# A matmul–bias–ReLU–matmul kernel: all block sums of y on VectorE, one product passed to the next through PSUM

## The chip, the cores and the metric

The kernel runs on one core of a Trainium2 chip. The core has five engines that run side by side, each through its own queue in order: TensorE (PE; its weight loads are shown apart as PEld), VectorE (DVE), ScalarE (ACT), GpSimd (POOL) and SyncE (SP), which issues most of the transfers. The metric is device time in microseconds for one execution. Before the change the median of three runs is 971.6 us (971.56 to 972.17).

## The reference

With x of 16 × 512 × 768, w1 of 768 × 3072, b1 of 3072 and w2 of 3072 × 768, all drawn at random in fp32:

```python
y = np.matmul(x, w1) + b1
y = np.maximum(y, 0)
return np.matmul(y, w2).astype(np.float32)
```

The 16 × 512 rows are one matrix of 8192 rows. The hidden width 3072 lies between the two products.

## The kernel before

**Tiling.** The rows are cut into 8 blocks of 1024 (`NSB`), the hidden width into 2 halves (`NCH`). So there are 16 iterations: 0 to 7 do the first half of the hidden width for the eight row blocks, 8 to 15 the second half, whose results are added in HBM to those of the first by accumulating DMAs that GpSimd issues. Operands are fp16, sums in PSUM fp32.

**First product, m1.** Each iteration forms y from x and w1 in six groups t = 0 to 5 (`first`, lines 524 to 583). A group is a 2 × 2 block product done in seven products instead of eight (Strassen–Winograd form): p1, p2, p6, p5, p7, p3, p4. Each is 3 matmuls of 128 × 512, so an iteration has 126 of them (line 537). The sums of x that they need (`sums_x`: slots XS1, XS2, XS4) and those of w1 (`sums_w1`: T1 to T4) are made ahead. Between the products ScalarE copies running sums with the bias to the SBUF tile `s` (`copy`, line 545: slots s1 = 0, s2 = 1 or 2, s5 = 4), and VectorE adds a bank to such a copy, clamps at 0 and writes y (`add`, line 549). p4 goes through ScalarE's Relu alone (line 579). Banks: kind "a" has three PSUM banks, "b" two, "c" three, and the group number picks the one. p6, p7 and p4 go on summing in p1's bank, p3 in p5's. Iteration 0 has a plain form of eight products instead (`first_plain`).

**Second product, m2.** Each iteration forms the output block from y and w2 in 20 products (`second`, list `SECOND`), each 8 matmuls of 128 × 384 (line 596). Products work on 20 blocks of y, of which 12 come out of m1 and the others are sums of blocks, and on 18 blocks of w2 and its sums. The y sums are eight instructions per quarter s of the columns (`sums_y`, line 458, two blocks each, 128 × 512 in all), four quarters. The quarters are complete after groups 1, 2, 4 and 5. Results go through ScalarE (line 612) and VectorE (line 618) into four output buffers `o` and to HBM. The same tile `s` holds m2's sums; its slot 4 is `s4`, last read by the 20th product's total, o6.

**Order.** All is written out by hand in one list (`run`, lines 699 to 726): each step has a key, and the steps are issued in the order of their keys. A group's seven steps have keys two apart and groups start seven apart, so the last three steps of a group lie between the first four of the next. m2's 20 steps follow two apart; its first step lies before the last two steps of group 5, and its last step after the first step of the next iteration's group 0. After every step up to two instructions are taken from the list `fill` (one during m2, unless more than eight wait), which holds the y sums of quarters 2 and 3, and then the step's `hooks` run, which `plan` fills: sums of x and w, squares for a range check (`stat_w1`, `stat_w2`, `square_x`), loads and stores.

**Where the y sums run.** `group_done` sends quarters 0 and 1 to GpSimd (`sums_y_aside`; in iteration 0 to VectorE) and quarters 2 and 3 through `fill` to VectorE. In iteration 7 the three sums of x for iteration 8 run on GpSimd (line 776). w1's sums run on GpSimd: in iteration 0 for the first half (24 instructions, lines 747 and 749), in iterations 1 to 6 for the second half, one group each, in borrowed x slots (`ahead_w1`). w2's 16 sums (`sum_w2`, line 329) run on VectorE and one of them on ScalarE.

Of the kernel before, what the change touches and what calls it, by code (L numbers as in the profile page):

```python
# [18 lines left out]
P = 128  # L19
# [130 lines left out]
class Fast:  # L150
# [32 lines left out]
    def __init__(self, ctx, tc, xf, w1, b1, w2, of):  # L183
        self.tc, self.nc = tc, tc.nc
        self.xf, self.w1, self.b1, self.w2, self.of = xf, w1, b1, w2, of
        self.M, self.K = xf.shape
        self.H, self.N = w2.shape
        self.NH = self.N // 2
        self.NSB = self.M // (2 * self.MH)
        self.NIT = self.NCH * self.NSB  # L190
        assert self.K == 6 * P and self.H == self.NCH * 2 * self.TP * P

        def pool(name, bufs, **kw):
            return ctx.enter_context(tc.tile_pool(name=name, bufs=bufs, **kw))
# [16 lines left out]
        self.w2dram = self.dram.tile([P, 6, 4, self.NH], FP16, name="w2d")  # L211
# [97 lines left out]

    def fetch_w2(self, slot, n=2):  # L310
        self.nc.sync.dma_start(out=self.v[:, slot:slot + n], in_=self.w2dram[:, slot:slot + n])

    def fetch_w2_aside(self, q):
        w = self.raw_pool.tile([P, 2, 4, self.NH], FP16, name="w2r", tag="raw")
        self.nc.sync.dma_start(out=w, in_=self.w2dram[:, 2 * q:2 * q + 2])
        self.w2_raw[2 * q], self.w2_raw[2 * q + 1] = w[:, 0], w[:, 1]

    def sum_w2(self, n):
# [3 lines left out]
        def block(slot):  # L322
            return self.w2_raw.get(slot, self.v[:, slot])

        if i is None:
            self.nc.scalar.activation(out=self.v[:, o], in_=block(j), func=ACTF.Copy,
                                      scale=float(sign))
        else:
            self.nc.vector.tensor_tensor(out=self.v[:, o], in0=block(i), in1=block(j),  # L329
                                         op=ALU.add if sign > 0 else ALU.subtract)  # L330
# [44 lines left out]

    def sums_x(self, it, which, engine=None):

        x = self.x.rearrange("p a k m -> p a (k m)")
        a11 = 4 * (it % 2)
        a12, a21, a22 = a11 + 1, a11 + 2, a11 + 3  # L380
        tt = (engine or self.nc.vector).tensor_tensor
        if which == 0:
            tt(out=x[:, self.XS1], in0=x[:, a21], in1=x[:, a22], op=ALU.add)
        elif which == 1:
            tt(out=x[:, a21:self.XS2 + 1:self.XS2 - a21],
               in0=x[:, a21:self.XS1 + 1:self.XS1 - a21],
               in1=x[:, a11:a11 + 1].to_broadcast((P, 2, 3 * self.MH)), op=ALU.subtract)
        else:
            tt(out=x[:, self.XS4], in0=x[:, a12], in1=x[:, self.XS2], op=ALU.subtract)

# [55 lines left out]

    def sums_y(self, n, s0, s1, engine=None):

        outs, ins0, ins1, sign = SUMS_Y[n]
        w = (s1 - s0) * self.QM  # L450

        def pair(i, j):
            cols = slice(s0 * self.QM, s1 * self.QM)
            if i == j:
                return self.y[:, i:i + 1, cols].to_broadcast((P, 2, w))
            return self.y[:, i:j + 1:j - i, cols]

        (engine or self.nc.vector).tensor_tensor(  # L458
            out=pair(*outs), in0=pair(*ins0), in1=pair(*ins1),
            op=ALU.add if sign > 0 else ALU.subtract)  # L460

    def group_done(self, it, t):

        def put(s0, s1, engine):
            self.fill += [lambda n=n: self.sums_y(n, s0, s1, engine) for n in range(8)]

        if t == 1:
            self.sums_y_aside(0, it)
        elif t == 2:
            self.sums_y_aside(1, it)  # L470
        elif t == 4:
            put(2, 3, self.nc.vector)
        elif t == 5:
            put(3, 4, self.nc.vector)

    def sums_y_aside(self, s, it):
        for n in range(8):
            self.sums_y(n, s, s + 1, self.nc.gpsimd if it else self.nc.vector)

    def first_plain(self, t):  # L480
# [34 lines left out]
        def last():  # L515
            step("a", m2, b2, 1, 1)
            self.group_done(0, t)

# [5 lines left out]
    def first(self, it, t):  # L524
# [22 lines left out]
        def add(half, m, ps, name):  # L547
# [3 lines left out]
                                  s1=0.0)  # L551

        def p1():
# [23 lines left out]
        def p4():  # L577
            mm(g["a"], xa22, self.T4, False)
            nc.scalar.activation(out=self.y_of(t, 1), in_=self.two(g["a"]), func=ACTF.Relu,  # L579
                                 bias=bias1)  # L580
            self.group_done(it, t)

        return [p1, p2, p6, p5, p7, p3, p4]


# [85 lines left out]
    def run(self):  # L671
# [42 lines left out]
        for _, n, i in sorted(keys):  # L714
# [13 lines left out]
    def plan(self):  # L728

        TP, NSB, NIT = self.TP, self.NSB, self.NIT  # L730
        self.hooks = {}
        pool = self.nc.gpsimd

# [14 lines left out]
        for t in range(TP):  # L748
            put("p1", 0, 5, 3, lambda t: self.sums_w1(self.w1s[t], (3,)), t)
        for n in range(len(SUMS_W)):  # L750
            put("p1", 0, 4 + n // 8, n % 8 // 2, self.sum_w2, n)

        for it in range(NIT):
            nxt = it + 1
            if nxt < NSB:
                for half in range(2):
                    if it:
                        put("m1", it, 1 + half, 0, self.transpose_x, nxt, half)
                    for s in range(4):
# [4 lines left out]
                put("m2", it, 0, 16, self.save_x, nxt, 0)  # L764
                put("m2", it, 0, 16, self.save_x, nxt, 1)
            elif nxt < NIT:
                put("m1", it, 0, 0, self.fetch_x, nxt, 0)
                if nxt > NSB:
                    put("m2", it, 0, 1, self.fetch_x, nxt, 1)
            if nxt < NSB:  # L770
                for n in range(3):
                    put("m2", it, 0, 8 + 2 * n, self.sums_x, nxt, n)

        last = NSB - 1
        for n in range(3):
            put("m2", last, 0, 1, self.sums_x, NSB, n, pool)
        for t in range(TP):
            for step, i in enumerate((0, 3, 8)):
                put("m2", 1 + t, 0, 1 + i, self.ahead_w1, 1 + t, t, step)
            put("m1", last, t, 6, self.fetch_w1, t)  # L780
        for n in range(12):
            put("m1", 1 + n // 3, 3 + n % 3, 0, self.load_w2,
                self.w2dram[:, n // 4 * 2:n // 4 * 2 + 2], 1, n // 4, n % 4)
        put("m1", last, 1, 6, self.fetch_w2_aside, 2)
        put("m1", last, 3, 6, self.fetch_w2_aside, 0)
        put("m2", last, 0, 9, self.fetch_w2, B0, 1)
        put("m2", last, 0, 13, self.fetch_w2, B2)
        for n, at in ((1, ("m2", last, 0, 6)), (2, ("m2", last, 0, 7)),
                      (7, ("m2", last, 0, 9)), (0, ("m2", last, 0, 11)),
                      (9, ("m2", last, 0, 12)), (15, ("m2", last, 0, 17)),  # L790
                      (3, ("m1", NSB, 0, 3)), (4, ("m1", NSB, 1, 1)), (5, ("m1", NSB, 1, 2)),
                      (6, ("m1", NSB, 1, 3)), (8, ("m1", NSB, 2, 1)), (10, ("m1", NSB, 2, 3)),
                      (11, ("m1", NSB, 3, 1)), (12, ("m1", NSB, 3, 3)),
                      (13, ("m1", NSB, 4, 1)), (14, ("m1", NSB, 4, 3))):
            put(*at, self.sum_w2, n)
# [61 lines left out]
```

## Time and profile before

| | |
|---|---|
| median of three runs | 971.6 us |
| profiled execution, its run | 976.38 us |
| its span, first to last instruction | 974.7 us |
| PE busy | 891.1 us, 91% |
| DVE busy | 653.2 us, 67% |
| ACT busy | 485.1 us, 50% |
| POOL busy | 472.8 us, 49% |

A row of a group of instructions names line, engine, operation, tiles, shapes and count, then the busy time, the mean of one in ns, and the idle time of the engine just before them with what ended it. In the timeline a row starts with the start in us and the length of a merged run of like instructions, and ends in brackets with the engine's idle time before it. A row of waits gives the total in us, the number of times and the longest. A row of stretches gives, behind its length, for each engine busy us and instruction count, then the share of the TensorE clock that was granted, the DMA share and GB/s. Ends of matmuls are modelled: a run of matmuls reads some 0.16 us longer than the distance to the next one's start.

### The profile page before, as it was taken

The page shows a single profiled execution, that of the slowest core. Times are in us where ns is not written, and L with a number is a line of the kernel's source. Part 1 is how long each engine was busy: PE and PEld are TensorE (multiplying, and loading weights), DVE is VectorE, ACT ScalarE, POOL GpSimd, SP SyncE. Part 2 cuts the span into 40 slices and gives each one's busy share as a digit, 9 for nine tenths or more (in the row PEclk, how much of TensorE's full clock was granted, in tenths as well). Part 3 has the DMA queues.
Part 4 walks back from the last instruction along what each step waited for, and adds up shares of the span by engine and source line. Part 5 has one row for each costly group of instructions (what it writes and reads, how often), then busy time and mean ns, then how long its engine had stood idle before and what let it go on. Part 6 is the DMA issues. An engine that isn't in the chain of part 4 may idle for free.

```text
span 974.7 us, 12785 instructions
## 1 busy us (share of the span) xinstructions
PE 891.1 (91%) x4677; PEld 463.7 (48%) x4677; DVE 653.2 (67%) x866; ACT 485.1 (50%) x731; POOL 472.8 (49%) x433
## 2 busy tenths in 40 slices
PE   8839989898998999999499999999989899999993
PEld 5315454453544545454254544545454454545452
DVE  2797585776748678584889757566475756657573
ACT  4615565655766556575235565566524334252430
POOL 6850743708255180725707364473625547372643
PEclk9969999999999999999799999999999999999997
DMA  9928769495895949649251563825356382634617
GB/s 201 197 89 216 164 119 299 58 323 98 167 262 63 335 52 272 129 116 388 84 180 64 146 97 114 130 73 107 65 144 100 114 127 78 118 52 84 95 17 115
DMA packets 120183, 137.73 MB, mean 141 GB/s; under 512 B 67101, under 2 KB 113717, under 8 KB 116277
## 3 DMA queue, kind: packets, MB, share of 16 engines
q0 software_dynamic: 50672, 46.41, 33.8%
q1 hardware_dynamic: 69120, 89.67, 29.0%
q8 instruction: 38, 0.62, 0.2%
q10 hardware_dynamic: 324, 0.80, 0.2%
q14 instruction: 29, 0.23, 0.1%
HBM read 71.77 MB, written 77.66 MB: 153 GB/s over the span
## 4 chain that ended last, share of the span: by engine, by line
PE 67%; DVE 14%; issue 9%; POOL 5%; ACT 2%; DMA 1%; DVEq 0%; POOLq 0%; ACTq 0%
PE ps L596 35%; PE ps L537 31%; DVE y L458 9%; POOL y L458 4%; DVE y L549 3%; DVE v L329 2%; POOL out_dram L627 1%; ACT y L579 1%; DMA out_dram<-o 1%; DMA w1s<-in_w_dram 1%; PE ps L489 1%; ACT s L545 1%; ACT scrap L373 0%; ACT y L494 0%; DVE x L430 0%
## 5 line engine op out<-in xcount | busy, mean ns | idle before, releaser
L596 PE MATMUL ps<-v,y 128*128 128x384 f16 x2560 | 441.5, 334 | 32.7 <-DVE y L458 21.2
L537 PE MATMUL ps<-x,w1s 128*128 128x512 f16 x1890 | 423.6, 381 | 32.8 <-DVE y L549 31.4
L458 POOL TENSOR_TENSOR y<-y 128x512 f16<-128x512 f16 x240 | 280.6, 1189 | 245.9 <-DVE y L549 171.9
L596 PEld LDWEIGHTS <-y 128*128 128x128 f16 x2560 | 255.2, 100 | 218.5 <-DVE y L458 24.6
L537 PEld LDWEIGHTS <-w1s 128*128 128x128 f16 x1890 | 184.9, 98 | 256.9 <-issue 42.9
L549 DVE CUSTOM_DVE_ANT_0 y<-ps,s 128x512 f16<-128x512 f32 x270 | 175.8, 686 | 158.5 <-ACT s L545 117.2
L545 ACT ACTIVATE s<-ps,b1y 128x512 f32<-128x512 f32 x270 | 179.5, 686 | 199.0 <-PE ps L537 184.5
L458 DVE TENSOR_TENSOR y<-y 128x512 f16<-128x512 f16 x272 | 185.6, 709 | 16.6 <-ACT y L494 10.4
L627 POOL DMA_DIRECT2D out_dram<-o x64 | 77.4, 1263 | 172.0 <-DVE o L618 169.8
L612 ACT ACTIVATE s<-ps 128x768 f32<-128x768 f32 x96 | 77.7, 810 | 143.9 <-PE ps L596 128.7
L618 DVE TENSOR_TENSOR s<-ps,s 128x768 f32<-128x768 f32 x96 | 90.1, 952 | 24.4 <-ACT s L612 11.6
L618 DVE TENSOR_TENSOR o<-s,ps 128x768 f32<-128x768 f32 x64 | 61.0, 954 | 58.2 <-PE ps L596 35.4
L579 ACT ACTIVATE y<-ps,b1y 128x512 f16<-128x512 f32 x90 | 61.8, 687 | 75.2 <-PE ps L537 75.0
L618 DVE TENSOR_TENSOR o<-ps,s 128x768 f32<-128x768 f32 x64 | 60.0, 955 | 34.7 <-ACT s L612 22.2
L373 ACT ACTIVATE scrap<-xn 128x768 f16<-128x768 f16 x60 | 50.3, 838 | 0.8
L285 POOL TENSOR_TENSOR x<-x 128x384 f16<-128x384 f16 x24 | 23.5, 990 | 27.5 <-DMA x<-in_w_dram 26.6
L337 ACT ACTIVATE scrap<-scrap 128x1536 f16<-128x1536 f16 x24 | 35.4, 1476 | 0.1
L612 ACT ACTIVATE ps<-ps 128x768 f32<-128x768 f32 x32 | 25.5, 798 | 10.2 <-PE ps L596 10.2
L285 POOL TENSOR_TENSOR w1s<-w1s 128x384 f16<-128x384 f16 x24 | 29.4, 1244 | 1.0
L360 POOL DMA_DIRECT2D xn<-in_x_dram x15 | 11.5, 769 | 36.6 <-ACT scrap L373 36.4
L489 PE MATMUL ps<-x,w1s 128*128 128x512 f16 x132 | 28.8, 379 | 0.4 <-DVE x L430 0.2
L329 DVE TENSOR_TENSOR v<-v 128x1536 f16<-128x1536 f16 x20 | 28.0, 1426 | 0.1
(63 smaller groups left out, 243.2 us busy)
## 6 DMA issues: line engine op xcount, KB each, us to landing
out_dram<-o SPq DMA_DIRECT2D x64, 384.0 KB, 6.9
out_dram<-o POOLq DMA_DIRECT2D x64, 384.0 KB, 6.1
xd<-x SPq DMA_DIRECT2D x8, 1536.0 KB, 6.2
x<-xd SPq DMA_DIRECT2D x8, 1536.0 KB, 7.2
xn<-in_x_dram POOLq DMA_DIRECT2D x15, 768.0 KB, 10.0
xd<-x SPq DMA_DIRECT2D x7, 1152.0 KB, 9.8
x<-xd SPq DMA_DIRECT2D x7, 1152.0 KB, 5.3
w1d<-x SPq DMA_DIRECT2D x6, 672.0 KB, 8.8
```

The lines of the kernel that those rows point to most:

```text
L285: self.nc.gpsimd.tensor_tensor(out=w[:, o], in0=w[:, i], in1=w[:, j], op=ALU.subtract)
L329: self.nc.vector.tensor_tensor(out=self.v[:, o], in0=block(i), in1=block(j), op=ALU.add if sign > 0 else ALU.subtract)
L373: self.nc.scalar.activation(out=self.junk(self.K), in_=rows, func=ACTF.Square, accum_out=self.stat[:, i:i + 1])
L458: (engine or self.nc.vector).tensor_tensor(out=pair(*outs), in0=pair(*ins0), in1=pair(*ins1), op=ALU.add if sign > 0 else ALU.subtract)
L537: nc.tensor.matmul(ps, lhsT=w[:, slot, k, :], rhs=x[:, xslot, k, :], start=(start and k == 0), stop=(k == 2), skip_group_check=True)
L545: nc.scalar.activation(out=kept(name), in_=ps, func=ACTF.Identity, bias=bias)
L549: nc.vector._custom_dve(TENSOR_ADD_SAT, out=self.y_of(self.TP * half + t, m), in0=self.two(ps), in1=self.two(kept(name)), s0=F_MAX, s1=0.0)
L579: nc.scalar.activation(out=self.y_of(t, 1), in_=self.two(g["a"]), func=ACTF.Relu, bias=bias1)
L596: nc.tensor.matmul(self.ps[:, 2 * q + j, 0:NH], lhsT=self.y[:, U_OF[p], m0:m0 + P], rhs=self.v[:, V_OF[p], s, :], start=(start and s == 0) ...
L612: nc.scalar.activation(out=o, in_=ps, func=ACTF.Copy, scale=float(sign))
L618: nc.vector.tensor_tensor(out=o, in0=a, in1=b, op=ALU.add if sign == kept_sign else ALU.subtract)
L627: nc.gpsimd.dma_start(out=rows, in_=o, accum_op=ALU.add)
```

## The change

- All y sums go through `fill` to VectorE, and `fill` is drained at one instruction a step in m1's groups 0 to 4 and late in m2, at two elsewhere.
- In groups 2 to 5 of `first`, ScalarE puts P1 plus bias into the bank of P2 (a write to PSUM in place of SBUF), P2's matmuls go on summing there, and ScalarE's Relu takes the result to y; VectorE's addition for P2 falls away. Groups 0 and 1 keep the old form.
- The seven products are issued in the order p1, p5, p6, p2, p7, p3, p4.
- Of the three sums of x, the double one (`which == 1`) goes to GpSimd and the others to VectorE, in iterations 0 to 7 alike, at m2's steps 6, 7 and 14.
- w1's fourth sum of the first half moves behind a step of m2 of iteration 0; w2's sums 8 to 15 of the first half move into m2 of iteration 0; those of the second half are spread anew, one pair of w2 blocks being fetched into free x slots.
- Transposing loads, w1's staging sums and stores, and fetches of x are moved by some steps.

```diff
     def fetch_w2_aside(self, q):
-        w = self.raw_pool.tile([P, 2, 4, self.NH], FP16, name="w2r", tag="raw")
+        if q == 1:
+            w = self.x[:, 4:6].rearrange("p a k m -> p (a k m)")
+        else:
+            w = self.raw_pool.tile([P, 8 * self.NH], FP16, name="w2r", tag="raw")
...
-    def sums_x(self, it, which, engine=None):
+    def sums_x(self, it, which):
...
         if which == 0:
-            tt(out=x[:, self.XS1], in0=x[:, a21], in1=x[:, a22], op=ALU.add)
+            self.nc.vector.tensor_tensor(out=x[:, self.XS1], in0=x[:, a21], in1=x[:, a22],
+                                         op=ALU.add)
         elif which == 1:
-            tt(out=x[:, a21:self.XS2 + 1:self.XS2 - a21],
+            self.nc.gpsimd.tensor_tensor(
+                out=x[:, a21:self.XS2 + 1:self.XS2 - a21],
...
         else:
-            tt(out=x[:, self.XS4], in0=x[:, a12], in1=x[:, self.XS2], op=ALU.subtract)
+            self.nc.vector.tensor_tensor(out=x[:, self.XS4], in0=x[:, a12],
+                                         in1=x[:, self.XS2], op=ALU.subtract)
...
-    def group_done(self, it, t):
-
-        def put(s0, s1, engine):
-            self.fill += [lambda n=n: self.sums_y(n, s0, s1, engine) for n in range(8)]
-
-        if t == 1:
-            self.sums_y_aside(0, it)
-        elif t == 2:
-            self.sums_y_aside(1, it)
-        elif t == 4:
-            put(2, 3, self.nc.vector)
-        elif t == 5:
-            put(3, 4, self.nc.vector)
...
+    def group_done(self, t):
+
+        s = {1: 0, 2: 1, 4: 2, 5: 3}.get(t)
+        if s is not None:
+            self.fill += [lambda n=n: self.sums_y(n, s) for n in range(8)]
...
+        seeded = t >= len(self.BANKS["b"])
+
...
         def p1():
             mm(g["a"], xa11, self.B11, True)
-            copy("s1", g["a"], bias1)
+            if seeded:
+                nc.scalar.activation(out=g["b"], in_=g["a"], func=ACTF.Identity, bias=bias1)
+            else:
+                copy("s1", g["a"], bias1)
 
         def p2():
-            mm(g["b"], xa12, self.B21, True)
-            add(0, 0, g["b"], "s1")
+            mm(g["b"], xa12, self.B21, not seeded)
+            if seeded:
+                relu(0, 0, g["b"])
+            else:
+                add(0, 0, g["b"], "s1")
...
-        return [p1, p2, p6, p5, p7, p3, p4]
+        return [p1, p5, p6, p2, p7, p3, p4]
...
-            for _ in range(2 if kind != "m2" or len(self.fill) > 8 else 1):
+            fast = kind == "p1" or (q == TP - 1 if kind == "m1" else i < 3)
+            for _ in range(2 if fast else 1):
                 if self.fill:
                     self.fill.pop(0)()
...
         for t in range(TP):
-            put("p1", 0, 5, 3, lambda t: self.sums_w1(self.w1s[t], (3,)), t)
-        for n in range(len(SUMS_W)):
-            put("p1", 0, 4 + n // 8, n % 8 // 2, self.sum_w2, n)
+            put("m2", 0, 0, 4, lambda t: self.sums_w1(self.w1s[t], (3,)), t)
+        for n in range(8):
+            put("p1", 0, 4, n // 2, self.sum_w2, n)
+        for n, at in ((9, ("p1", 0, 5, 2)), (8, ("m2", 0, 0, 2)), (12, ("m2", 0, 0, 4)),
+                      (10, ("m2", 0, 0, 5)), (14, ("m2", 0, 0, 7)), (13, ("m2", 0, 0, 9)),
+                      (11, ("m2", 0, 0, 11)), (15, ("m2", 0, 0, 12))):
+            put(*at, self.sum_w2, n)
...
-            if nxt < NSB:
-                for n in range(3):
-                    put("m2", it, 0, 8 + 2 * n, self.sums_x, nxt, n)
+            if nxt <= NSB:
+                for n, i in enumerate((6, 7, 14)):
+                    put("m2", it, 0, i, self.sums_x, nxt, n)
+            elif nxt < NIT:
+                put("m2", it, 0, 1, self.fetch_x, nxt, 1)
 
         last = NSB - 1
-        for n in range(3):
-            put("m2", last, 0, 1, self.sums_x, NSB, n, pool)
         for t in range(TP):
-            for step, i in enumerate((0, 3, 8)):
-                put("m2", 1 + t, 0, 1 + i, self.ahead_w1, 1 + t, t, step)
+            for step, at in enumerate((("m2", 1 + t, 0, 1), ("m2", 1 + t, 0, 13),
+                                       ("m1", 2 + t, 0, 3))):
+                put(*at, self.ahead_w1, 1 + t, t, step)
...
+        for n, at in ((2, ("m2", last, 0, 12)), (6, ("m2", last, 0, 14)),
+                      (1, ("m2", last, 0, 16)), (15, ("m2", last, 0, 17)),
+                      (3, ("m1", NSB, 0, 3)), (9, ("m1", NSB, 1, 1)), (7, ("m1", NSB, 1, 2)),
+                      (0, ("m1", NSB, 1, 3)), (8, ("m1", NSB, 2, 1)), (5, ("m1", NSB, 2, 3)),
+                      (12, ("m1", NSB, 3, 1)), (10, ("m2", NSB, 0, 5)),
+                      (14, ("m2", NSB, 0, 6)), (4, ("m2", NSB, 0, 7)),
+                      (13, ("m2", NSB, 0, 11)), (11, ("m2", NSB, 0, 14))):
             put(*at, self.sum_w2, n)
```

More of the change, by code (lines that the diff above doesn't have):

```diff
@@ L210, in __init__ @@
         self.w1dram = [self.dram.tile([P, 7, 3, P], FP16, name=f"w1d{t}") for t in range(self.TP)]
-        self.w2dram = self.dram.tile([P, 6, 4, self.NH], FP16, name="w2d")
+        self.w2dram = self.dram.tile([P, 6, 4 * self.NH], FP16, name="w2d")
         self.scrap = self.one.tile([P, 4 * self.NH], FP16, name="scrap")
@@ L322, in block @@
         def block(slot):
-            return self.w2_raw.get(slot, self.v[:, slot])
+            return self.w2_raw.get(slot, self.v[:, slot].rearrange("p s n -> p (s n)"))
+        out = self.v[:, o].rearrange("p s n -> p (s n)")
         if i is None:
-            self.nc.scalar.activation(out=self.v[:, o], in_=block(j), func=ACTF.Copy,
+            self.nc.scalar.activation(out=out, in_=block(j), func=ACTF.Copy,
                                       scale=float(sign))
         else:
-            self.nc.vector.tensor_tensor(out=self.v[:, o], in0=block(i), in1=block(j),
+            self.nc.vector.tensor_tensor(out=out, in0=block(i), in1=block(j),
                                          op=ALU.add if sign > 0 else ALU.subtract)
@@ L445, in two, with sums_y @@
         return ps.rearrange("p (a m) -> p a m", a=2)
[L447 removed]
+    def sums_y(self, n, s):
         outs, ins0, ins1, sign = SUMS_Y[n]
[L450 removed]
+        cols = slice(s * self.QM, (s + 1) * self.QM)
         def pair(i, j):
[L453 removed]
             if i == j:
[L455 removed]
+                return self.y[:, i:i + 1, cols].to_broadcast((P, 2, self.QM))
             return self.y[:, i:j + 1:j - i, cols]
[L458 to L478 removed]
+        self.nc.vector.tensor_tensor(out=pair(*outs), in0=pair(*ins0), in1=pair(*ins1),
+                                     op=ALU.add if sign > 0 else ALU.subtract)
+    def group_done(self, t):
+        s = {1: 0, 2: 1, 4: 2, 5: 3}.get(t)
+        if s is not None:
+            self.fill += [lambda n=n: self.sums_y(n, s) for n in range(8)]
     def first_plain(self, t):
@@ L516, in last @@
             step("a", m2, b2, 1, 1)
-            self.group_done(0, t)
+            self.group_done(t)
         rest = [lambda: step("b", m2, b1, 0, 1), last]
@@ L551, in add, with relu @@
                                   s1=0.0)
+        def relu(half, m, ps, **kw):
+            nc.scalar.activation(out=self.y_of(self.TP * half + t, m), in_=self.two(ps),
+                                 func=ACTF.Relu, **kw)
         def p1():
             mm(g["a"], xa11, self.B11, True)
-            copy("s1", g["a"], bias1)
+            if seeded:
+                nc.scalar.activation(out=g["b"], in_=g["a"], func=ACTF.Identity, bias=bias1)
+            else:
+                copy("s1", g["a"], bias1)
         def p2():
-            mm(g["b"], xa12, self.B21, True)
-            add(0, 0, g["b"], "s1")
+            mm(g["b"], xa12, self.B21, not seeded)
[3 more added lines that the diff above has]
+                add(0, 0, g["b"], "s1")
         def p6():
@@ L578, in p4 @@
             mm(g["a"], xa22, self.T4, False)
-            nc.scalar.activation(out=self.y_of(t, 1), in_=self.two(g["a"]), func=ACTF.Relu,
-                                 bias=bias1)
-            self.group_done(it, t)
-        return [p1, p2, p6, p5, p7, p3, p4]
+            relu(0, 1, g["a"], bias=bias1)
+            self.group_done(t)
+        return [p1, p5, p6, p2, p7, p3, p4]
     def second(self, it):
@@ L731, in plan @@
         self.hooks = {}
-        pool = self.nc.gpsimd
         def put(kind, it, q, i, fn, *args):
@@ L757, in plan @@
                     if it:
-                        put("m1", it, 1 + half, 0, self.transpose_x, nxt, half)
+                        put("m1", it, 2 + half, 0, self.transpose_x, nxt, half)
                     for s in range(4):
@@ L782, in plan @@
             put("m1", 1 + n // 3, 3 + n % 3, 0, self.load_w2,
[L783 to L786, printed above, removed]
-        put("m2", last, 0, 13, self.fetch_w2, B2)
[L788 to L794, printed above, removed]
+                self.w2dram.rearrange("p b (s n) -> p b s n", s=4)[:, n // 4 * 2:][:, 0:2], 1,
+                n // 4, n % 4)
+        for q, at in ((2, ("m1", last, 1, 6)), (0, ("m1", last, 3, 6)), (1, ("m2", last, 0, 1))):
+            put(*at, self.fetch_w2_aside, q)
+        put("m2", last, 0, 9, self.fetch_w2, B0)
+        put("m2", last, 0, 13, self.fetch_w2, B2)
+        for n, at in ((2, ("m2", last, 0, 12)), (6, ("m2", last, 0, 14)),
[5 more added lines that the diff above has]
+                      (13, ("m2", NSB, 0, 11)), (11, ("m2", NSB, 0, 14))):
             put(*at, self.sum_w2, n)
```

17 lines of the change are left out of this document (9 added, 8 removed).

## The prediction

> **What bounds the kernel now.** I read first who keeps TensorE waiting, then the length of iterations, then the timeline of an ordinary iteration and of the long one.
>
> ```profile
> core 0 of [0], span 974.7 us
> engine line waited for: us in total, times, longest us
> PE ps L537 <- DVE y L549: 31.4, 16, 3.2
> PE ps L596 <- DVE y L458: 21.2, 2, 10.9
> ...
> PE ps L596 <- DVE stat L654: 1.1, 1, 1.1
> PE ps L596 <- DVE flag L664: 1.0, 1, 1.0
> ```
>
> TensorE is the bound, and nearly all its waits end on VectorE: once an iteration before p4 of the last group (the product that goes on in the bank that p7's addition, line 549, still reads), and twice, long, on y sums. The stretches of iterations 0, 4, 7, 13 and 15 with the tail:
>
> ```profile
> 0.00:91.82 91.82, 69.40 (x375) 39.12 (x376) 61.66 (x75) 41.59 (x74) 53.17 (x68) 0.91 0.94 163
> 266.78:324.99 58.21, 55.21 (x289) 28.42 (x287) 40.50 (x53) 35.40 (x56) 27.41 (x27) 0.97 0.77 186
> 437.71:505.71 68.00, 55.72 (x288) 28.57 (x286) 49.80 (x56) 23.65 (x33) 30.91 (x19) 0.92 0.56 204
> 793.22:848.31 55.09, 53.53 (x287) 27.81 (x286) 34.93 (x51) 22.14 (x32) 28.15 (x25) 1.00 0.53 108
> 903.46:974.70 71.24, 54.99 (x295) 28.53 (x293) 37.65 (x53) 22.15 (x32) 33.06 (x28) 0.93 0.49 73
> ```
>
> The same 286 matmuls take 58.21 us at a granted clock of 0.97, or 55.09 at 1.00. Where the waits are:
>
> ```profile
> 241.03 1.38 PE L537 MATMUL ps<-x,w1s 128*128 128x512 f16 x3 [2.99 <-DVE y L549]
> ...
> 234.53 5.85 DVE L458 TENSOR_TENSOR y<-y 128x512 f16<-128x512 f16 x4
> ...
> 230.62 9.47 POOL L458 TENSOR_TENSOR y<-y 128x512 f16<-128x512 f16 x8
> ...
> 795.17 25.42 PE L537 MATMUL ps<-x,w1s 128*128 128x512 f16 x117
> ...
> 823.96 0.81 PE L537 MATMUL ps<-x,w1s 128*128 128x512 f16 x3 [1.43 <-DVE y L549]
> 824.60 23.87 PE L596 MATMUL ps<-v,y 128*128 128x384 f16 x144
> ```
>
> In iteration 3 p4 waits 2.99 us, since p7's addition stands on VectorE behind four y sums that took 5.85 us while GpSimd did its own. The prices of one instruction alone:
>
> ```profile
> L458 DVE TENSOR_TENSOR y<-y x272: 407/424/6080, 17.8 to 943.9; 128x512 f16<-128x512 f16 x136
> L458 POOL TENSOR_TENSOR y<-y x240: 1141/1156/1875, 99.3 to 933.3; 128x512 f16<-128x512 f16 x120
> ```
>
> A y sum is 0.42 us on VectorE, yet 1.46 in that queue and 6.08 at worst: it stands until GpSimd's instruction is done.
>
> **An iteration without a wait.** In iteration 13 a matmul of m1 takes 25.42/117 = 0.217 us and one of m2 23.87/144 = 0.166, a short wait included. Its 55.09 us less p4's wait (1.43 + 0.16 of modelled end) and 0.3 of a shorter wait on a y sum leave **53.2 us**. Iteration 4 loses 5.0 against that: some 3.2 of wait, as in iteration 3 (2.99 + 0.16), and 1.5 to 1.8 of slow clock (58.21 × 0.03 = 1.7). The wait of 1.43 cost no clock, those near 3 did; eight iterations have one of the long kind. By the Trainium skill, "TensorE: Matmul & The Clock Gate", section "What's actually happening", half rate comes after an idle window of about 3.4 us; by that rule alone the 3 us waits would cost no clock, and the change would save no clock, some 8 × 1.5 = 12 us less, and come out at 943 us. The rows' 0.97 and 1.00 do not agree with so long a window, and they decide; 943 lies inside the forecast's own range and gets no chance beside it.
>
> **y sums.** 16 instructions of 1.156 us leave GpSimd in each of 15 iterations and add 16 × 0.42 = 6.7 us to VectorE, which loses four additions of p2 (line 549) and the stand behind GpSimd:
>
> ```profile
> L549 DVE CUSTOM_DVE_ANT_0 y<-ps,s 128x512 f16<-128x512 f32 x270 | 175.8, 686 | 158.5 <-ACT s L545 117.2
> L545 ACT ACTIVATE s<-ps,b1y 128x512 f32<-128x512 f32 x270 | 179.5, 686 | 199.0 <-PE ps L537 184.5
> ...
> L612 ACT ACTIVATE ps<-ps 128x768 f32<-128x768 f32 x32 | 25.5, 798 | 10.2 <-PE ps L596 10.2
> ```
>
> VectorE in iteration 4 becomes 40.5 + 6.7 − 4 × 0.69 − some 3 of standing − the double x sum, under 41 of 53.2 us: no bound. In a group of m1 (7 products of 0.65 = 4.5 us) it has at most two additions and seven sums, 2 × 0.69 + 7 × 0.42 = 4.3. For the end of m1, count from the end of group 4's p4. Relu for it is done at 0.9 (0.2 to start, 0.69). The second and third sum of quarter 2 follow, to 1.7; p7 of group 5 ends at 1.3, so its addition runs to 2.4. TensorE does p2, p7, m2's first product and p3 until 0.65 + 0.65 + 1.3 + 0.65 = 3.25 and finds the bank free: **p4's wait goes**, with 0.8 us to spare. The next sum due, U15 for m2's third product, is done at 5.6 and needed at 6.2.
>
> **The seed.** P1 into P2's bank is the same ScalarE instruction with another destination. At this size no row shows it; writing 768 columns of PSUM takes 798 ns, and 512 into SBUF 686, so I take 0.69 (0.6 to 0.8). ScalarE gets 4 × 0.69 = 2.7 us more per iteration, 38 of 53, and five instructions per group, 3.4 of 4.5 us. With a square for the range check between (16 groups) it is 0.3 us late for p6: **+4.8** (0 to 9).
>
> **The new order, and what it brings forward.** p5 moves from fourth to second place. Its copy goes to slot 4 of `s`, which is m2's `s4` until o6, the last total, has read it. Two boundaries:
>
> ```profile
> 270.58 0.95 DVE L618 TENSOR_TENSOR o<-s,ps 128x768 f32<-128x768 f32 x1 [0.93 <-DMA out_dram<-o]
> ...
> 271.65 1.27 ACT L545 ACTIVATE s<-ps,b1y 128x512 f32<-128x512 f32 x2 [0.73 <-DVE o L618]
> ...
> 741.14 0.95 DVE L618 TENSOR_TENSOR o<-s,ps 128x768 f32<-128x768 f32 x1 [3.31 <-DMA out_dram<-o]
> ...
> 742.21 1.27 ACT L545 ACTIVATE s<-ps,b1y 128x512 f32<-128x512 f32 x2 [2.42 <-DVE o L618]
> ```
>
> o6 itself waits for an output buffer. Against the start of m2's last matmul (268.57) it ends at +2.96, at the second one at +4.65; at all fifteen between +1.3 and +4.65, mean 2.6. Now p5's copy is third among ScalarE's copies there and nothing stands behind it in need. After the change it is second, and p6's copy, without which p7 may not go on in its bank, stands behind it. p7 is due at 0.16 + 4 × 0.65 = +2.75 (p5, p6, p2, next p1); p6's copy ends 0.1 + 0.65 + 0.7 = 1.45 after o6. **A new wait of 2.6 + 1.45 − 2.75 = 1.3 us on average** (0 to 3.4), 19.4 over fifteen, and 1.5 of clock at the one of 3.4: **20.9** (5 to 35; o6's moment may move either way, as stores of w1 leave that stretch and a load of x enters it).
>
> **The x sums.** Iteration 7 has all three on GpSimd:
>
> ```profile
> 472.11 6.04 POOL L385 TENSOR_TENSOR x<-x 128x3072 f16<-128x3072 f16 x1
> ```
>
> Behind this one VectorE's y sum stood 6.08 us, and TensorE 10.9. After the change the same instruction runs in iterations 0 to 7, but at m2's step 7, some 9 to 15 us into m2, when the last y sums (two a step until step 2, then one, so gone at step 4) are done. Its result is wanted by the third x sum at step 14, 18 us in: hidden. If a y sum were still queued it would cost up to 6 us. In iteration 7 only a w2 sum can meet it, 0.5 us at most; so **iteration 7 falls from 68.0 to 53.2**.
>
> **Iteration 0.**
>
> ```profile
> 32.05 30.39 POOL L285 TENSOR_TENSOR w1s<-w1s 128x384 f16<-128x384 f16 x24
> ...
> 67.50 3.23 PE L596 MATMUL ps<-v,y 128*128 128x384 f16 x10 [10.30 <-DVE y L458]
> 72.10 3.15 PE L596 MATMUL ps<-v,y 128*128 128x384 f16 x17 [1.37 <-ACT s L612]
> ```
>
> Before U15's y sum five w2 sums are taken out of VectorE's queue; m2's fifth product then starts near 65 instead of 72.1. (GpSimd's 24 w1 sums stay back to back until 62.4: moving the last six behind a later step puts nothing before them on GpSimd's queue.) But the w2 sums come back inside m2, and two of them (14 and 13) meet GpSimd's x sum of 6.04 us, put there by the change; the output totals queued behind them then hold m2's fourteenth product some 4.5 us, plus clock. I take **no gain** (−7 to +1).
>
> **Queues.** GpSimd's second load of x is issued behind the x sum, 2 us later, with over 10 us in hand; SyncE's transposes wait for w1's store, now in the next m1, and must be landed only by m2's step 6. Both I cost at nothing; uncovered they would hold m2's x sums, not the products before.
>
> **The sum**, on the profile's 974.7: iteration 0 91.8; iterations 1 to 14 14 × 53.2 = 744.8; iteration 15 with its tail 71.24 less 1.9 as in iteration 13, 69.3; boundaries 20.9; squares 4.8; the two waits of the range check 2.1, which stay. Total **933.7**, 41 less. The three runs' median lies 3.1 below that span: **931 us**.
>
> **The rivals.**
>
> - *The boundary costs nothing*: o6 is done at +1.3, as at three of the fifteen boundaries now. Against it: at twelve it waits on a buffer, and nothing frees that earlier. 931 − 21 = 910, down to 903 with iteration 0's gain. Chance 0.16.
> - *p4's wait stays*, since the added sums keep VectorE late at the end of m1. For it: 4.3 of 4.5 us in the groups before; against it: quarter 1 is drained before group 5 begins. At 1.9 per iteration, as in iteration 13, 15 × 1.9 = 28: 959. Chance 0.14.
> - *Slower, by the boundary*: o6 at +4.65 every time, so 3.35 of wait and 1.5 of slow clock, 15 × 4.85 = 73 in place of 21: 983. It decides from a total of 62, 4.1 a boundary, o6 at about +3.9. Against it: one boundary in fifteen does so now. Chance 0.04.
> - *The change does not take GpSimd out of VectorE's way*: the long x sum meets y sums in iterations 0 to 7. The Trainium skill, "SBUF — State Buffer", section "Who interferes with whom", has the second to issue of a VectorE instruction with two SBUF inputs and a GpSimd one that reads SBUF stand for the whole of the other; the 6.08 us row agrees. At some 6 us each, 8 × 6 = 48: 979. Against it: the y sums end five steps earlier. Chance 0.04.
>
> **How the numbers follow.** The forecast has 0.62; its own range, from the bounds of boundary, squares and iteration 0, is 915 to 946. The range 905 to 952 takes in most of the first rival and the near side of the second (a wait that stays in part). No change means within 0.2%, 2 us, about what a measurement of this kernel can tell. Faster holds the forecast and the first two rivals, 0.92; slower the last two but for a sliver, 0.07.
>
> **What would show it.** Right: no wait of line 537 on line 549 at the end of m1; a granted clock of 1.00 in iterations 1 to 14 but for one or two; a wait of line 537 on ScalarE's copies (line 545's successor) about 1.3 us long at most boundaries; iteration 7 as long as its neighbours; y sums at 0.42 us; an iteration 0 of 85 to 93 us. Wrong: TensorE waiting on y sums or on additions within m1's groups 1 to 4 (VectorE too full), or o6 waiting longer than now.

## The result, and the profile after

The changed kernel takes 931.3 us (930.3 to 933.3) against 971.9 us: a ratio of 0.958, with a 95% interval of 0.956 to 0.960. Its profiled execution spans 930.4 us, against 974.7 before.

Lines have new numbers after the change: 534 is m1's matmul, 602 m2's, 542 ScalarE's copies, 557 the seed, 551 the Relu, 546 VectorE's additions, 466 the y sums, 624 VectorE's totals, 336 the w2 sums, 392 the double x sum. Who keeps TensorE waiting, in the changed kernel:

```profile
PE ps L534 <- ACT s L542: 14.2, 9, 2.5
PE ps L602 <- DVE v L336: 7.5, 2, 7.0
PE ps L602 <- DVE y L466: 6.0, 1, 6.0
PE ps L534 <- DVE o L624: 5.1, 8, 3.0
PE ps L602 <- DVE o L624: 3.6, 1, 3.6
```

The wait on additions (31.4 us before, on line 549) is gone altogether. In its place stands one on ScalarE's copies, 14.2 us. The three rows of line 602 all lie in iteration 0. The y sums, in the form of the row of prices before:

```profile
L466 DVE TENSOR_TENSOR y<-y x512: 409/419/1576, 17.9 to 898.8; 128x512 f16<-128x512 f16 x171
```

The middle one of the three times is the median. All 512 y sums now run on VectorE, and the longest takes 1.58 us where it was 6.08. The stretches of iterations 0, 4, 7, 13 and 15 with the tail (columns as before):

```profile
0.00:92.42 92.42, 71.83 (x375) 39.91 (x376) 64.89 (x74) 41.78 (x74) 60.11 (x72) 0.89 0.97 169
255.13:310.52 55.39, 53.55 (x286) 27.93 (x286) 37.39 (x65) 37.43 (x60) 12.80 (x9) 1.00 0.83 196
417.66:472.07 54.41, 53.35 (x286) 27.89 (x286) 39.56 (x67) 26.14 (x37) 6.00 (x1) 1.00 0.75 285
749.57:804.59 55.02, 53.36 (x289) 27.92 (x286) 35.92 (x63) 24.55 (x36) 9.66 (x9) 1.00 0.52 108
859.84:930.40 70.56, 54.81 (x295) 28.62 (x293) 38.34 (x65) 24.55 (x36) 14.48 (x12) 0.93 0.50 75
```

Between the first matmul of one iteration and that of the next, summed by kind:

| iterations | before, us | after, us | difference |
|---|---|---|---|
| 0 | 91.8 | 92.4 | +0.6 |
| 1 to 6 | 345.9 | 325.2 | −20.7 |
| 7 | 68.0 | 54.4 | −13.6 |
| 8 to 14 | 397.7 | 387.8 | −10.0 |
| 15 and tail | 71.3 | 70.5 | −0.8 |

Only iteration 0 gains nothing. The granted clock is 1.00 from iteration 1 to 14. The end of m1 in iteration 4, VectorE's timeline and then TensorE's:

```profile
283.78 0.76 DVE L466 TENSOR_TENSOR y<-y 128x512 f16<-128x512 f16 x2 [0.89 <-ACT y L551]
284.45 0.69 DVE L546 CUSTOM_DVE_ANT_0 y<-ps,s 128x512 f16<-128x512 f32 x1
285.05 1.67 DVE L466 TENSOR_TENSOR y<-y 128x512 f16<-128x512 f16 x4
```

```profile
284.15 1.46 PE L602 MATMUL ps<-v,y 128*128 128x384 f16 x8
285.45 1.46 PE L534 MATMUL ps<-x,w1s 128*128 128x512 f16 x6
286.74 0.49 PE L602 MATMUL ps<-v,y 128*128 128x384 f16 x2
```

p7's addition starts at 284.45 behind two y sums that took 0.76 us, where, in iteration 3 before, four took 5.85; the six matmuls of p3 and p4 run on without a gap. The boundary into iteration 4, VectorE, ScalarE and TensorE:

```profile
259.10 0.95 DVE L624 TENSOR_TENSOR o<-s,ps 128x768 f32<-128x768 f32 x1 [2.29 <-DMA out_dram<-o]
...
260.17 1.84 ACT L542 ACTIVATE s<-ps,b1y 128x512 f32<-128x512 f32 x3 [3.51 <-DVE o L624]
...
261.49 1.89 PE L534 MATMUL ps<-x,w1s 128*128 128x512 f16 x8 [1.66 <-ACT s L542]
```

o6 waits for an output buffer, p5's copy for o6, p6's copy stands behind p5's, and p7 waits for that.

In iteration 0 the long x sum meets the w2 sums, as VectorE, GpSimd and TensorE show:

```profile
74.17 6.99 DVE L336 TENSOR_TENSOR v<-v 128x1536 f16<-128x1536 f16 x2
...
73.48 5.99 POOL L392 TENSOR_TENSOR x<-x 128x3072 f16<-128x3072 f16 x1 [3.17 <-DVE x L389]
...
82.07 10.51 PE L602 MATMUL ps<-v,y 128*128 128x384 f16 x48 [3.61 <-DVE o L624]
```

Two w2 sums, each 0.95 us elsewhere, take 6.99 us beside GpSimd's one, and the fourteenth product waits for the totals behind them.

### The profile page after: what moved, and what is told of

It reads as the page before. It is cut to its first block, busy times and chain, and to the rows that moved or that the text cites. A ratio compares the mean times of both kernels' runs of the same rounds, so it can differ in the third digit from the quotient of the medians.

```text
span 930.4 us, 12569 instructions
## 1 busy us (share of the span) xinstructions
PE 875.0 (94%) x4677; PEld 459.9 (49%) x4677; DVE 630.7 (68%) x1041; ACT 519.0 (56%) x791; POOL 224.8 (24%) x198
## 4 chain that ended last, share of the span: by engine, by line
PE 42%; issue 36%; DVE 8%; POOL 7%; DMA 4%; ACT 2%; POOLq 0%; DVEq 0%; ACTq 0%
PE ps L534 22%; PE ps L602 18%; POOL out_dram L633 7%; DMA out_dram<-o 4%; DVE o L624 2%; DVE v L336 2%; DVE y L466 2%; DVE ps L624 1%; DMA w1s<-in_w_dram 1%; PE ps L484 1%; ACT s L618 1%; ACT s L542 0%; ACT scrap L380 0%; ACT y L489 0%; DVE x L439 0%
## 5 line engine op out<-in xcount | busy, mean ns | idle before, releaser
L602 PE MATMUL ps<-v,y 128*128 128x384 f16 x2560 | 430.6, 329 | 17.3 <-DVE v L336 7.5
L534 PE MATMUL ps<-x,w1s 128*128 128x512 f16 x1890 | 417.0, 379 | 20.3 <-ACT s L542 14.2
L602 PEld LDWEIGHTS <-y 128*128 128x128 f16 x2560 | 251.4, 99 | 193.6 <-issue 11.0
L466 DVE TENSOR_TENSOR y<-y 128x512 f16<-128x512 f16 x512 | 212.0, 440 | 41.7 <-ACT y L551 26.3
L542 ACT ACTIVATE s<-ps,b1y 128x512 f32<-128x512 f32 x210 | 141.6, 687 | 172.1 <-PE ps L534 61.0
L546 DVE CUSTOM_DVE_ANT_0 y<-ps,s 128x512 f16<-128x512 f32 x210 | 144.9, 690 | 106.2 <-PE ps L534 73.6
L624 DVE TENSOR_TENSOR s<-ps,s 128x768 f32<-128x768 f32 x96 | 90.2, 953 | 12.6 <-ACT s L618 6.5
L392 POOL TENSOR_TENSOR x<-x 128x3072 f16<-128x3072 f16 x8 | 48.0, 6004 | 71.4 <-DVE x L389 71.4
L277 POOL DMA_DIRECT2D x<-in_w_dram x12 | 10.1, 848 | 163.7 <-PE ps L534 163.7
L557 ACT ACTIVATE ps<-ps,b1y 128x512 f32<-128x512 f32 x60 | 39.6, 659 | 10.8 <-PE ps L534 7.9
L551 ACT ACTIVATE y<-ps 128x512 f16<-128x512 f32 x60 | 35.8, 597 | 0.0
L484 PE MATMUL ps<-x,w1s 128*128 128x512 f16 x132 | 28.8, 379 | 0.4 <-DVE x L439 0.2
```

Of the source, the lines that this page charges most:

```text
L392: self.nc.gpsimd.tensor_tensor(out=x[:, a21:self.XS2 + 1:self.XS2 - a21], in0=x[:, a21:self.XS1 + 1:self.XS1 - a21], in1=x[:, a11:a11 + 1] ...
L466: self.nc.vector.tensor_tensor(out=pair(*outs), in0=pair(*ins0), in1=pair(*ins1), op=ALU.add if sign > 0 else ALU.subtract)
L534: nc.tensor.matmul(ps, lhsT=w[:, slot, k, :], rhs=x[:, xslot, k, :], start=(start and k == 0), stop=(k == 2), skip_group_check=True)
L542: nc.scalar.activation(out=kept(name), in_=ps, func=ACTF.Identity, bias=bias)
L546: nc.vector._custom_dve(TENSOR_ADD_SAT, out=self.y_of(self.TP * half + t, m), in0=self.two(ps), in1=self.two(kept(name)), s0=F_MAX, s1=0.0)
L551: nc.scalar.activation(out=self.y_of(self.TP * half + t, m), in_=self.two(ps), func=ACTF.Relu, **kw)
```

## The experiments

Each kernel was timed in a group of runs together with the kernel before, on one chip. The kernel before had medians of 971.9, 974.3, 972.0 and 973.3 us in the four groups, so a difference of 2 or 3 us between kernels of different groups is not clear of noise. The times below stand against the 931.3 us of the changed kernel.

**The slot of p5's copy.**

```diff
-        slots = {"s1": 0, "s2": 1 + t % 2, "s5": 4}
+        slots = {"s1": 0, "s2": 1 + t % 2, "s5": 5}
```

> The changed kernel with p5's copy in slot 5 of s, which m2's eighteenth product's total frees, in place of slot 4. Theory (p7's wait at each boundary comes from the copy of p5 standing behind o6 on slot 4): the waits of line 534 on ScalarE's copies, 14.2 us, vanish, and with the modelled ends 16.9 us go: 931 to 914 us. Rival (o6's wait for an output buffer holds VectorE, and so p7 and p4, whatever the slot): 929 to 931 us, and line 534 waits on VectorE's line 546 instead.

915.5 us (915.1 to 916.4). TensorE's waits:

```profile
PE ps L602 <- DVE v L336: 7.3, 2, 7.0
PE ps L602 <- DVE y L466: 6.3, 1, 6.3
PE ps L534 <- DVE o L624: 4.9, 8, 2.8
PE ps L602 <- DVE o L624: 3.8, 1, 3.8
```

The copies have left the list, and nothing took their place. So the new wait comes from the slot, and costs 15.8 us.

**GpSimd's long x sum in iteration 0.** Only iteration 0's double sum goes to VectorE.

```diff
         elif which == 1:
-            self.nc.gpsimd.tensor_tensor(
+            (self.nc.vector if it == 1 else self.nc.gpsimd).tensor_tensor(
```

> The changed kernel with the double x sum of iteration 0 alone on VectorE. Theory (two w2 sums stand behind GpSimd's 6 us and hold the totals behind them): the wait of 3.6 us before m2's fourteenth product of iteration 0 goes, with half of 6.8 us at half clock: iteration 0 from 92.4 to about 86.5, 926 us. Rival (VectorE is full there anyway, the sum takes 1.75 us of its own): 930 to 931 us.

928.5 us (926.5 to 931.4); iteration 0 takes 88.0 us in place of 92.4, and its wait of 3.6 us before the fourteenth product is gone, with shorter ones in its place (1.2 at most). The theory holds for the iteration, at 4.4 instead of 5.9 us; in the total the two kernels' runs overlap, so the gain of 2.9 us is not shown there.

**The y sums alone.** The kernel before, with this and nothing else:

```diff
-        if t == 1:
-            self.sums_y_aside(0, it)
-        elif t == 2:
-            self.sums_y_aside(1, it)
...
+        s = {1: 0, 2: 1, 4: 2, 5: 3}.get(t)
+        if s is not None:
+            self.fill += [lambda n=n: self.sums_y(n, s, s + 1) for n in range(8)]
...
+            fast = kind == "p1" or (q == TP - 1 if kind == "m1" else i < 3)
+            for _ in range(2 if fast else 1):
```

> The kernel before with the y sums alone changed: all on VectorE through the list, drained as after the change; seed, order of products, x sums and w2 sums as before. Theory (GpSimd's y sums, which VectorE's stand behind, are the cause of p4's wait): p4's wait and its slow clock go without a wait at the boundary in their place, iterations 1 to 6 and 8 to 15 near 53.5, iteration 7 and iteration 0 as before: 926 us. Rival (without the seed VectorE is too full, three additions and seven sums of 4.5 to 5.0 us in groups of 4.5): TensorE waits on line 549 within groups 2 to 5, 945 us or more.

936.4 us (936.1 to 936.9), between the two, but not for the rival's reason. Stretches of iterations 4, 7 and 13, and TensorE in iterations 4 and 7:

```profile
258.40:314.56 56.16, 53.97 (x287) 27.78 (x286) 43.80 (x70) 35.38 (x56) 7.12 (x8) 1.00 0.79 197
424.29:488.09 63.80, 56.17 (x289) 28.84 (x287) 53.08 (x72) 23.63 (x33) 12.27 (x3) 0.92 0.60 217
759.05:812.68 53.63, 53.35 (x288) 27.90 (x286) 38.02 (x67) 22.12 (x32) 9.65 (x9) 1.00 0.54 111
```

```profile
293.40 2.77 PE L584 MATMUL ps<-v,y 128*128 128x384 f16 x16 [1.28 <-DVE y L458]
...
461.23 1.44 PE L525 MATMUL ps<-x,w1s 128*128 128x512 f16 x3 [7.63 <-DVE y L537]
```

Where GpSimd has no sums (iteration 13) an iteration takes 53.6 us, with three additions in every group: VectorE is not too full. What is left outside iteration 0 is, first of all, what GpSimd's other sums do: those of w1 early in m2, beside which four of VectorE's y sums take 3.60 us (a wait of 1.3 us in iterations 1 to 6), and the x sums of iteration 7 (7.6). Against the kernel before in its own group (974.3 us) this one part is worth 38 us; the whole change is worth 40.6.

**Without the seed**, the new order kept.

```diff
-        seeded = t >= len(self.BANKS["b"])
+        seeded = False
```

> The changed kernel without the seed: all groups in the old form (copy of P1 to slot 0, addition on VectorE), the new order of products kept. Theory (the seed makes the room on VectorE that the y sums need): a late addition in groups 2 to 5, some 0.5 us each in two or three groups of fifteen iterations, 940 to 955 us. Rival (VectorE had room): 931 us.

935.0 us (934.7 to 936.4), 3.7 more, though the ratios to the kernel before overlap (0.958 to 0.963 here, 0.956 to 0.960 for the changed kernel). No addition is late in ordinary iterations. Iteration 8, where w2 sums share VectorE, loses 0.8 us, and iterations 11 and 12, with the range check, 1.3 and 0.6; the rest moves with the boundaries. The seed is worth little, and VectorE had room without it.

**Iteration 7's x sums**, in the kernel before, on VectorE.

```diff
-            if nxt < NSB:
+            if nxt <= NSB:
                 for n in range(3):
                     put("m2", it, 0, 8 + 2 * n, self.sums_x, nxt, n)
...
-        for n in range(3):
-            put("m2", last, 0, 1, self.sums_x, NSB, n, pool)
```

> The kernel before with iteration 7's three x sums on VectorE at steps 8, 10 and 12, as its other iterations have them. Theory (GpSimd's long x sums were the whole of iteration 7's excess, through VectorE's y sums behind them): iteration 7 from 68.0 to about 55.1, the kernel 13 us shorter, 959 us. Rival (the w2 sums that only iteration 7 has are part of it): 62 us or more, the kernel at 965.

```profile
384.55:439.65 55.10, 53.56 (x288) 27.84 (x287) 38.82 (x54) 33.14 (x52) 24.10 (x22) 1.00 0.59 162
439.65:495.93 56.28, 53.95 (x288) 27.83 (x286) 41.85 (x59) 23.64 (x33) 18.48 (x16) 1.00 0.67 244
```

Iteration 7, the second line, takes 56.3 us, 11.7 less, near iteration 6's 55.1. The one time taken is 966.1 us, with 969.6 to 977.5 for the kernel before on that chip; profile against profile it is 964.4 and 974.7. Iteration 0 ran 1.6 us longer here and iteration 8 0.9, so the total leaves the size open and the iteration settles the cause.

**The long x sum early.** The first two x sums at m2's step 0.

```diff
-                for n, i in enumerate((6, 7, 14)):
+                for n, i in enumerate((0, 0, 14)):
```

> The changed kernel with the first two x sums, VectorE's and GpSimd's of 6 us, at m2's step 0 in place of 6 and 7, in all iterations 0 to 7. Theory (VectorE's fp16 sums stand for the whole of GpSimd's instruction, and only the late step hides that): quarter 3's y sums and the addition of p3 behind them are late by up to 6 us, TensorE waits 4 to 6 us in each of iterations 1 to 7, 960 to 980 us. Rival (the two share and slow each other): 1 to 2 us an iteration, 938 to 945 us.

987.3 us in the one run taken: slower than the kernel before. Iteration 2's m2 begins, on VectorE, GpSimd and TensorE:

```profile
185.32 6.63 DVE L466 TENSOR_TENSOR y<-y 128x512 f16<-128x512 f16 x3
...
185.03 5.98 POOL L392 TENSOR_TENSOR x<-x 128x3072 f16<-128x3072 f16 x1 [37.31 <-DVE x L389]
...
192.01 4.31 PE L602 MATMUL ps<-v,y 128*128 128x384 f16 x16 [5.62 <-DVE y L466]
```

Three y sums take 6.63 us beside a GpSimd instruction of 5.98, and TensorE waits 5.6; at half clock after it an iteration loses some 8 us. The theory holds; the loss is larger than expected, since each such wait takes the clock for 6.8 us in most iterations. The step at which these two sums stand is worth 56 us; the rows show that the long one does it.

**w1's sums of iteration 0 late**, with its x sum on VectorE.

```diff
-            put("p1", 0, max(t, 2), 3, lambda t: self.sums_w1(self.w1s[t], (0, 1, 2)), t)
-        for t in range(TP):
-            put("m2", 0, 0, 4, lambda t: self.sums_w1(self.w1s[t], (3,)), t)
...
+        for t in range(TP):
+            put("m2", 0, 0, 5 if t < 3 else 9, lambda t: self.sums_w1(self.w1s[t]), t)
```

> The changed kernel with iteration 0's double x sum on VectorE, and GpSimd's 24 sums of w1 put behind its load of x in m2 of iteration 0 (groups 0 to 2 at step 5, 3 to 5 at step 9), so that they no longer run beside VectorE's first y and w2 sums. Theory (iteration 0's waits of 7.0 and 6.0 us are VectorE's sums of 0.42 and 0.95 us standing at 1.07 and 1.6 behind GpSimd's): both waits go, less some 4 us given back inside m2, where w2's sums now meet them: iteration 0 from 88 to about 79, 919 us. Rival (the w2 loads or VectorE's amount of work set it): 926 to 929 us, as with the x sum alone.

918.1 us (916.4 to 920.1); iteration 0 and VectorE in it:

```profile
0.00:76.41 76.41, 67.24 (x375) 38.56 (x376) 47.33 (x75) 41.79 (x74) 44.39 (x61) 0.98 1.08 185
```

```profile
36.73 5.42 DVE L336 TENSOR_TENSOR v<-v 128x1536 f16<-128x1536 f16 x6 [2.06 <-DMA v<-in_w_dram]
42.07 0.75 DVE L466 TENSOR_TENSOR y<-y 128x512 f16<-128x512 f16 x2
```

In the changed kernel the same six sums read:

```profile
39.77 9.58 DVE L336 TENSOR_TENSOR v<-v 128x1536 f16<-128x1536 f16 x6
```

They take 5.42 us in place of 9.58, and iteration 0 falls by 11.6 us against the kernel with the x sum alone. The waits of 7.0 and 6.0 us were GpSimd's sums beside VectorE's. One new wait of 1.6 us comes in iteration 1, on one of the w1 sums that are now late.

**Together**: slot 5, iteration 0's x sum on VectorE, late w1 sums, and the third x sum at step 16, its store at 17.

```diff
-                for n, i in enumerate((6, 7, 14)):
+                for n, i in enumerate((6, 7, 16)):
...
-                put("m2", it, 0, 16, self.save_x, nxt, 1)
+                put("m2", it, 0, 17, self.save_x, nxt, 1)
```

> The changed kernel with p5's copy in slot 5, iteration 0's double x sum on VectorE, w1's 24 sums late, and the third x sum two steps later (16, its store at 17), so that the total o7 does not stand behind it. Theory: the gains add, 16 for the slot, 12 for iteration 0, 0.3 in each of iterations 1 to 6 before p1: 901 us. Rival (one wait hides another): 908 us or more.

899.1 us (898.3 to 900.3), less than either kernel: the gains add. Iterations 2, 3, 5 and 6 take 53.23 us in place of 53.57: what is gone is the wait of p1 on m2's total o7.

**The old order without the seed**, on top of all else in the change.

```diff
-        seeded = t >= len(self.BANKS["b"])
+        seeded = False
...
-        return [p1, p5, p6, p2, p7, p3, p4]
+        return [p1, p2, p6, p5, p7, p3, p4]
```

> The changed kernel without the seed and with the products in their old order (p1, p2, p6, p5, p7, p3, p4); the y sums, x sums and w sums stay as changed. Theory (seed and new order together cost what the boundary costs, and VectorE has room for the additions): no wait of 17 us in total at the boundaries, 1 to 3 us lost at single places where the additions are late, 917 us. Rival (the seed makes the room on VectorE): waits of TensorE on VectorE's additions in groups 2 to 5, 931 us or more.

918.8 us (916.9 to 920.0): 12.6 us less than the changed kernel. Its stretches of iterations 4 and 13:

```profile
252.70:306.52 53.82, 53.64 (x286) 27.90 (x286) 39.61 (x69) 35.38 (x56) 12.79 (x9) 1.00 0.85 202
742.34:795.53 53.19, 53.19 (x287) 27.93 (x286) 38.01 (x67) 22.13 (x32) 9.69 (x9) 1.00 0.54 112
```

In the change as it stands, seed and order together cost more than they bring. The slot makes the difference: with slot 5 the kernel with seed and new order takes 915.5 us. Whether the two bring anything then is not clear, as the ratios overlap (0.938 to 0.943 there, 0.939 to 0.948 here).

**The shortest version**: the version of 899 us with these edits besides.

```diff
-        for t in range(TP):
-            put("m2", 0, 0, 5 if t < 3 else 9, lambda t: self.sums_w1(self.w1s[t]), t)
+        for t in range(TP):
+            at = ("p1", 0, 2, 3) if t == 0 else ("m2", 0, 0, 9 if t < 4 else 14)
...
-                put("m2", it, 0, 8, self.fetch_x, nxt, 0)
+                put("m2", it, 0, 1, self.fetch_x, nxt, 0)
...
-                      (12, ("m1", NSB, 3, 1)), (10, ("m2", NSB, 0, 5)),
-                      (14, ("m2", NSB, 0, 6)), (4, ("m2", NSB, 0, 7)),
+                      (12, ("m1", NSB, 3, 1)), (10, ("m1", NSB, 4, 3)),
+                      (14, ("m1", NSB, 5, 0)), (4, ("m1", NSB, 5, 1)),
```

> The kernel with slot 5, iteration 0's double x sum on VectorE, the late third x sum and late w1 sums, and now w1's sums of group 0 early, of groups 1 to 3 at step 9 and of 4 and 5 at step 14 of iteration 0's m2, three w2 sums of iteration 8 moved from its m2 into groups 4 and 5 of its m1, and the fetch of iteration 9's x at step 1 in place of 8. Theory (before iteration 9 the total o7 waits for an output buffer because the totals before it are late and their transfers share the engines with the fetch): that wait of 3.1 us goes and iteration 0 loses 2 to 3 us less: 893 us. Rival (the buffer's transfer alone sets it): 897 to 899 us.

894.7 us (894.0 to 894.9), a ratio of 0.919 (0.915 to 0.922) to the kernel before. Iterations 0, 8 and 9:

```profile
0.00:76.51 76.51, 65.34 (x375) 37.72 (x376) 49.39 (x74) 41.79 (x74) 42.81 (x62) 1.00 1.12 196
450.03:504.52 54.49, 53.74 (x286) 27.87 (x286) 47.02 (x77) 33.05 (x44) 4.85 (x4) 1.00 0.45 131
504.52:557.71 53.19, 53.19 (x286) 27.90 (x286) 36.23 (x63) 37.16 (x52) 9.71 (x9) 1.00 0.55 111
```

Iteration 8 falls from 57.1 to 54.5 us: the wait before iteration 9 is gone. Which of the two causes named there did it, the late totals or the fetch, was not tried apart. Iteration 0 did not gain (75.8 us in the version of 899 us), against the expectation.

The moves of loads, transposes and stores that belong to the change were not tried apart.

## Why the prediction was right, point by point

- **p4's wait goes**: right. 31.4 us of waiting and the slow clock behind it disappear. The y sums alone bring it about in all iterations but 7 and 8, where 7.6 and 2.6 us of waiting on additions stay. VectorE in iteration 4 is busy 37.4 us (under 41 was forecast), ScalarE 37.4 (38).
- **The boundary**: right in place, cause and nearly in size: 16.9 us by the distances of matmul starts (19.4 forecast, and 1.5 of clock that did not come). The slot experiment shows the cause. The forecast was o6's end, counted from the start of m2's last matmul, less 1.3 us; in the changed kernel o6 ends at 1.32 us at four boundaries, where p7 waits for nothing, and at 1.62 to 3.99 at the other eleven, and there p7's wait is that number less 1.3 to within 0.03 us.
- **Iteration 7**: right, 54.4 us for 53.2; the rest, 1.2 us, is p1's wait at its end, for m2's total o7, which stands on VectorE behind the third x sum and a w2 sum.
- **Iteration 0**: right as taken, "no gain", and by the reason given. A y sum's wait of 10.3 us fell to 6.0, and the fourteenth product waits 3.6 us (4.5 forecast) behind totals that stand behind two w2 sums; taking the x sum away returns 4.4 us.
- **The seed**: its price was 0.66 us apiece for the 0.69 forecast. The 4.8 us for the squares of the range check, which were to make it late for p6, were wrong: iteration 5, with two of the squares, takes 53.6 us, as iterations 1 and 6 without them. And the rival that feared VectorE too full was argued from 4.3 of 4.5 us; without the seed and its relief it still is not the bound.
- **Missed**: p1's wait on o7. In iterations 1 to 6 the third x sum, now at m2's step 14 in place of 12, stands in front of o7 on VectorE (0.35 us each); before iteration 8 p1 waits 1.2 us, as said, and before iteration 9 o7 itself waits for an output buffer (3.1 us). That makes some 6.5 us. The two waits of the range check, 2.1 us, were kept in the sum and went.
- **The total**: the sum was 933.7 for a span of 930.4, and it is that near in part by luck: 4.0 us too much at the boundaries, 4.8 for the squares and 2.1 for the range check stand against the 6.5 that were missed. The 3.1 us taken off it for the median were the profile's own: before, the profiled run took 976.4 for a median of 971.9, after it 931.9 for 931.3. That the median came out at 931 owes something to the error of the sum and that of these 3.1 us having opposite signs.
- **The clock**: that it returns to 1.00 was right; what the prediction took to cost the clock was not. See the last section.

## What to carry to other kernels

A second engine that works beside VectorE on SBUF operands can cost more than it carries: look for VectorE's instructions that are long only when the other one runs, and price them by that row. When an instruction is moved forward in an engine's queue, follow the buffer that it writes back to its last reader in the stage before, and ask what stands behind it; here taking the next slot, free by then, was worth 15.8 us. A long GpSimd instruction belongs where nothing on VectorE is queued against it; the same sum seven steps earlier turned a gain of 40 us into a loss of 15.

## What was not expected of the hardware

The prediction took the length of a single wait for what costs TensorE its clock. The runs show another rule. In each of the twelve profiles the granted clock changes only at whole multiples of 3.41 us from its other changes, and it drops to one half after such a stretch in which TensorE was idle for most of the time. A grid stretch of the kernel before, at the wait ahead of p4 in iteration 9, and the one after:

```profile
592.69:596.10 3.41, 1.25 (x8) 0.54 (x7) 3.41 (x5) 0.00 (x0) 2.38 (x2) 1.00 0.36 81
596.10:599.51 3.41, 3.41 (x10) 1.46 (x10) 2.72 (x7) 1.39 (x2) 0.00 (x0) 0.50 0.98 326
```

And the same wait of p1 before iteration 9, about 3 us, in the changed kernel and in the one with slot 5:

```profile
524.16:527.58 3.42, 1.57 (x10) 0.83 (x9) 0.71 (x1) 0.00 (x0) 0.46 (x1) 1.00 1.03 209
527.58:530.99 3.41, 2.27 (x13) 1.26 (x13) 1.92 (x2) 0.69 (x1) 1.26 (x2) 1.00 1.17 202
```

```profile
519.84:523.25 3.41, 0.67 (x5) 0.29 (x3) 0.96 (x1) 0.00 (x0) 0.00 (x0) 1.00 1.09 192
523.25:526.67 3.42, 3.37 (x10) 1.43 (x10) 1.44 (x2) 0.69 (x1) 2.36 (x2) 0.50 1.17 203
```

In the first the wait falls across a grid line and costs no clock; in the second it falls within one stretch, and the next runs at half. In the twelve profiles, outside iteration 0 and the last iteration with its tail, every full-rate stretch with 2.03 us or more without a busy PE is followed by half rate (31 of them), and none with 1.99 or less; as the ends of matmuls are modelled, the true idle times are some 0.16 us longer for each wait. By the Trainium skill, "TensorE: Matmul & The Clock Gate", section "What's actually happening", the window is 3413 ns and runs free of the kernel, as here. It puts the drop after an idle window; by these traces the window need be idle only to some 60% (2.03 of 3.41 us). So whether a wait of 2 to 4 us costs the clock is a matter of where it falls: by these rows a shorter one does not fill a stretch far enough, and a longer one must do so on one side of a grid line. Iterations of the kernel before were near 17 stretches long (58.0 us), so their waits fell alike from one to the next. The kernel before also differs by a few us from run to run (969.6 to 977.5 us in one group, at granted clocks of 0.977 to 0.964); that this comes from where its waits fall on the grid is likely, and not shown.
